# Banks of their own for the small products of a nested fast multiplication, with the products in another order

## The chip, the cores and the metric

The kernel runs on one core of a Trainium2 chip. The time is that of the device for one execution, in microseconds (us). The kernel before was run three times: 2297.75, 2298.81 and 2299.09 us, median 2298.81. The engines are TensorE (PE in the profile, its weight loads PEld), VectorE (DVE), ScalarE (ACT), GpSimd (POOL) and SyncE (SP), which here only issues transfers.

## The reference

An encoder of two layers takes one inference step for a prompt of 1024 rows and a sample of 32 rows, 1056 columns of 1024 features in the kernel. Layer one mixes with a matrix memory, layer two with windowed attention. Each is followed by a feed-forward block, which is where the change lies:

```
def swiglu(x, w_gu, w_down):
    g, u = jnp.split(x @ w_gu, 2, axis=-1)
    return (jax.nn.silu(g) * u) @ w_down

x = layer_norm(DEEPNORM_ALPHA * x + swiglu(x, w_gu[layer], w_down[layer]), ...)
```

The inner width is 2816. All is float32. The kernel splits every float32 number into a high part and a low part and makes three matmuls of each product (high by high, high by low, low by high).

## The kernel before

**The products.** The up projection has 22 units of 128 inner rows a layer (`FT`). Most are computed with a fast 2 x 2 block scheme: seven products in place of eight. Each product, called by the weight factor and the operand it multiplies, is 4 blocks deep, 2 column groups of 264 wide and 3 matmuls a block: 24 matmuls of 128 x 128 by 128 x 264. Its factors are a1, a2, b2, s2, s1, s3, s4. Four of them (a1, s2, s1, s4) add up in one PSUM tile, A, which ScalarE copies out between them (`gate0`, `up0`, `up1`, and last the silu); the others go to a tile B, which VectorE adds to `up0` or `up1`.

**The doubles.** Sixteen pairs of neighbouring units, 8 pairs a layer (`DOUBLES`, function `up_double`), go further: two units are rows 0 and 1, and the two a2 products are replaced by a second, nested scheme of seven small products of 6 matmuls each. They use four weights: g1 (a chain and a side product), g2 and g3 (a chain and a side product each) and g4 (a chain product). The chain products add up in one PSUM bank. A side product has the other bank. After each, VectorE adds the bank to a quarter of a gate (line 1582). Both banks are the halves of one tile, `inner`.

**Who orders what.** Each engine works through its own queue in the order in which the program is written. A planner, `Weights`, holds a list of jobs (`self.jobs`): one job makes one factor. VectorE forms the sum if there is one (lines 194 to 197 for g2; 212 for b2, 215 and 216 for s2, 218 for s1), ScalarE casts the high part (line 244), GpSimd subtracts for the low part (line 246). Five slots hold factors. When a product is done its slot is free, and jobs are made until four slots are taken (`done`), so jobs run about four ahead of the products. Raw weights (`wr`, line 172) are loaded on SP when the last job of a unit pair is made; the nested weights of the next double (`wn`, line 185) when the job g4 is made, since there is one buffer.

**The stage.** Results of finished unit pairs are prepared for the down projection by a generator, `stage`: it forms sums on VectorE, casts on ScalarE (line 1383), splits on GpSimd or VectorE (line 1384) and stores (line 1385, `hs_x` and `hs_t`). It is woven between the products by a clock of nominal times: each block of three matmuls ticks 0.339 us, and `yield` gives the time to the next step. `rest` and `finish_tile` do the same for the silu and the products that close a unit. The steps of the first stage sum are in lines 1395 and 1396, its cast follows after `yield 2.0`; a later step adds to a sum in line 1401.

**PSUM.** A and B are made by `bank`, which alternates two names a tag (`A0`, `A1`, `B0`, `B1`), two banks each, eight in all. In the doubles `B1` is `inner`.

Of the kernel before, what the change touches and what calls it, by code (L numbers as in the profile page):

```python
# [13 lines left out]
PSUM = bass.MemoryType.PSUM  # L14
DRAM = bass.MemoryType.DRAM

P = 128
# [112 lines left out]
class Weights:  # L130
# [7 lines left out]
    def __init__(self, nc, pool, units, pairs, doubles, on_vector):  # L138
        self.nc, self.pool, self.units, self.on_vector = nc, pool, units, on_vector
        self.nload = self.njob = 0  # L140
        self.raw, self.parts, self.home, self.live = {}, {}, {}, set()
        self.jobs, self.last = [], {}
        self.wait, self.ahead, self.pause = 0.0, False, FEED_W
        self.depth = RAW - 1
        self.doubles, self.inner, self.nest, self.nfetch = doubles, {}, None, 0
        self.spare, self.spared = None, set()
        u = 0
        while u < len(units):
            if u in doubles:
                v = u + 2  # L150
                self.jobs += [(u, f) for f in ("a1", "b2", "s2", "g1", "s1", "s3", "s4")]
                self.jobs += [(v, f) for f in ("a1", "b2")] + [(u, "g2"), (v, "s2"), (u, "g3")]
                self.jobs += [(v, f) for f in ("s1", "s3")] + [(u, "g4"), (v, "s4")]
                for i in range(4):
                    self.last[u + i] = len(self.jobs) - 1
                u += 4
            elif u in pairs:
                self.jobs += [(u, f) for f in self.FACTORS]
                self.last[u] = self.last[u + 1] = len(self.jobs) - 1
                u += 2  # L160
            else:
                self.jobs += [(u, 0), (u, 1)]
                self.last[u] = len(self.jobs) - 1
                u += 1
# [125 lines left out]
def kernel(ctx: ExitStack, tc: tile.TileContext, A, O):  # L290
# [1019 lines left out]
    def ffn(layer, li, tasks, lx, final):  # L1310
# [10 lines left out]
        AB = slice(0, 2)  # L1321
        px = ExitStack()

        turns = {"A": 0, "B": 0}

        def bank(tag, one=None):
            i = turns[tag] if one is None else one
            turns[tag] = 1 - i
            return new(px.pool[tag], f"{tag}{i}", [P, 2, 512])[:, :, :N4]

        X = seven(E)
        extras = ("t2", "t3", "t4")
# [39 lines left out]
        def stage(p):  # L1372

            (s11, s12), (s21, s22) = (kept.pop(2 * p + i) for i in range(2))
            s33, *pairs_ = places_
            m = s33 and buf(s33)
            pause = 5.2

            def put(o, s, eng, last=False):
                i = pairs_[turn[0]][0]  # L1380
                turn[0] ^= 1
                hi, lo = buf(i), buf(i + 1)
                nc.scalar.copy(hi.bitcast(F32R), buf(s))
                eng.tensor_sub(lo.bitcast(F32R), buf(s), hi)  # L1384
                nc.sync.dma_start(hs[o][:, p], buf2(i))
                if last:
                    release(s)

            if p in BLOCKS[TAIL]:
                for i, (o, s) in enumerate((("x11", s11), ("x12", s12), ("x21", s21), ("x22", s22))):  # L1390
                    put(o, s, (nc.gpsimd, nc.vector)[i % 2], True)
                    yield 4.0
                return

            nc.vector.tensor_sub(m, buf(s22), buf(s12))
            nc.vector.tensor_sub(buf(s12), buf(s12), buf(s11))
            yield 2.0
            put("t1", s12, nc.gpsimd, True)
            yield pause
            put("t3", s33, nc.vector)  # L1400
            nc.vector.tensor_add(m, m, buf(s11))
# [159 lines left out]

        def up_double(i):
            us = up[i], up[i + 1]
            inner = bank("B", 1)
            chain, side = inner[:, 0], inner[:, 1]
            gate0, up0, up1 = [None] * 2, [None] * 2, [None] * 2
            slot = [{}, {}]

# [32 lines left out]
            for row in range(2):  # L1601
                a = bank("A")
                mul(row, a, "a1", "x11")
                finish_tile()
                gate0[row] = take(row, "g0")
                nc.scalar.copy(gate0[row], a)
                if not row:
                    staging.append(wv.launch(stage(i // 2 - 1)))
                b = bank("B", 0)
                mul(row, b, "b2", "t4")  # L1610
                if row:
                    small(chain, "g2", 1, "t2", [(1, 0)], True, False)
                    small(side, "g2", 0, "t3", [(1, 1)])
                mul(row, a, "s2", "t2", again=True)
                up0[row] = take(row, "u0")
                nc.scalar.copy(up0[row], a)
                nc.vector.tensor_add(up0[row], up0[row], b)
                if row:
                    small(chain, "g3", 0, "t1", [(1, 1)], True, False)
                    small(side, "g3", 1, "t4", [(1, 0)], True)  # L1620
                else:
                    small(chain, "g1", 0, "x11", [(0, 0)], False, False)
                    small(side, "g1", 1, "x21", [(0, 0)])
                mul(row, a, "s1", "t1", again=True)
                up1[row] = take(row, "u1")
                nc.scalar.copy(up1[row], a)
                b = bank("B", 0)
                mul(row, b, "s3", "t3")
                nc.vector.tensor_add(up0[row], up0[row], b)
                nc.vector.tensor_add(up1[row], up1[row], b)  # L1630
                if row:
                    small(chain, "g4", 0, "x22", [(0, 1)], True)
                mul(row, a, "s4", "x22", again=True)
                nc.scalar.activation(take(row, "s1"), a, AF.Silu)
                tail.append(wv.launch(rest(row)))

# [74 lines left out]
        for i in range(FIRST, FT):  # L1711
            if i in DOUBLES:
                while nests:
                    wv.drain(nests.pop())
                up_double(i)
            elif i - 1 not in DOUBLES:
                if i == FIRST + 1:
                    open_nested()
                if i == DOUBLES.stop:
                    close_nested()  # L1720
# [529 lines left out]
```

## Time and profile before

| what | us |
|---|---|
| median of three runs | 2298.81 |
| profiled execution, its own time | 2297.69 |
| its span | 2295.9 |
| TensorE busy | 2188.7 |
| VectorE busy | 1534.3 |
| GpSimd busy | 1052.9 |
| ScalarE busy | 1020.0 |

A row of a timeline gives start, duration, engine, line, operation, out<-in and, in brackets, how long the engine had been idle and what ended that. A row of the waits gives who waited for whom, total us, times and the longest. A row of stretches gives the busy time of each engine between two moments, then the clock that TensorE was granted and the DMA's share and rate. Matmuls are pipelined: each shows about 0.28 us, but they start 0.12 us apart.

### The profile page before, as it was taken

Reading aid. Unit: us, or ns where it says so; the run is one execution under the profiler, and the core shown is the slowest. Engines: PE = TensorE matmul, PEld = TensorE weight load, DVE = VectorE, ACT = ScalarE, POOL = GpSimd, SP = SyncE. Lnnn points to the kernel's source line nnn. Section 1 sums busy time; section 2 is a strip of 40 time slices with the busy share of each in tenths; the row PEclk is TensorE's granted clock in tenths of the full one; section 3 lists DMA queues with packets and bytes.
Section 4 is the critical chain, followed back from the end, with each engine's and each line's share of the span. In section 5 each row is a group of like instructions: output and inputs, shape, how many; then the busy total and the mean of one; then the engine's idle time right before and its main releaser. Section 6 shows DMA issues by size and latency. Waiting matters only on the chain. (4 is left out here: it accounts for less than half of the span.)

```text
span 2295.9 us, 44506 instructions
## 1 busy us (share of the span) xinstructions
PE 2188.7 (95%) x16990; PEld 2150.8 (94%) x16990; DVE 1534.3 (67%) x3008; ACT 1020.0 (44%) x2299; POOL 1052.9 (46%) x1014
## 2 busy tenths in 40 slices
PE   9999999999898989999999999999889898999997
PEld 9999999999898989999998999899889898999997
DVE  4465677787576666566667778887766666556657
ACT  4443445464443434322246778665434343432224
POOL 2544200005665656454526777402565656554441
PEclk9999999999999999999999999999999999999999
DMA  4222214122434343697515434402443434399622
GB/s 164 76 59 68 59 31 142 28 83 98 155 134 159 129 144 146 231 336 244 179 66 170 118 90 114 156 27 93 141 153 130 144 136 158 113 347 302 209 83 76
DMA packets 181413, 315.15 MB, mean 137 GB/s; under 512 B 18832, under 2 KB 131528, under 8 KB 181200
## 3 DMA queue, kind: packets, MB, share of 16 engines
q1 hardware_dynamic: 176848, 307.98, 40.4%
q10 hardware_dynamic: 4352, 4.33, 0.6%
q8 instruction: 134, 2.20, 0.4%
q14 instruction: 79, 0.65, 0.1%
HBM read 214.51 MB, written 87.27 MB: 131 GB/s over the span
## 5 line engine op out<-in xcount | busy, mean ns | idle before, releaser
L246 POOL TENSOR_TENSOR wl_s<-wr,wh_s 128x512 fp32r<-128x512 f32 x224 | 317.6, 1433 | 282.8 <-ACT wh_s L244 219.9
L412 PE MATMUL d<-sx,wh 128*128 128x264 f32 (+2 forms) x1068 | 341.7, 320 | 2.5 <-ACT wh L244 2.4
L414 PE MATMUL d<-sx,wl 128*128 128x264 f32 (+2 forms) x1068 | 325.9, 305 | 2.3 <-POOL wl L246 2.3
L413 PE MATMUL d<-sx,wh 128*128 128x264 f32 (+2 forms) x1068 | 325.2, 304 | 0.4 <-DVE sx L443 0.4
L246 POOL TENSOR_TENSOR wl_a<-wr,wh_a 128x512 fp32r<-128x512 f32 x80 | 108.5, 1357 | 402.8 <-ACT wh_a L244 401.9
L244 ACT CAST wh_s<-wr 128x512 fp32r<-128x512 f32 x224 | 134.7, 618 | 317.3 <-DVE wr L216 257.9
L412 PE MATMUL A<-sx,wh_s 128*128 128x264 f32 x896 | 259.3, 289 | 2.7 <-ACT z L1467 2.7
L413 PE MATMUL A<-sx,wh_s 128*128 128x264 f32 x896 | 258.7, 289 | 0.0
L414 PE MATMUL A<-sx,wl_s 128*128 128x264 f32 x896 | 258.6, 289 | 0.0
L412 PEld LDWEIGHTS d<-sx,wh 128*128 128x128 f32 x1068 | 201.9, 189 | 6.0 <-ACT wh L244 3.2
L414 PEld LDWEIGHTS d<-sx,wl 128*128 128x128 f32 x1068 | 201.5, 189 | 3.7 <-POOL wl L246 3.4
L413 PEld LDWEIGHTS d<-sx,wh 128*128 128x128 f32 x1068 | 202.2, 189 | 1.6 <-DVE sx L443 0.7
L412 PE MATMUL d<-sx,ex 128*128 128x264 f32 x624 | 180.5, 289 | 0.1
L413 PE MATMUL d<-sx,ex 128*128 128x264 f32 x624 | 177.2, 284 | 0.0
L414 PE MATMUL d<-sx,ex 128*128 128x264 f32 x624 | 176.9, 284 | 0.0
L412 PEld LDWEIGHTS A<-sx,wh_s 128*128 128x128 f32 x896 | 173.1, 193 | 3.1 <-ACT z L1467 3.1
L414 PEld LDWEIGHTS A<-sx,wl_s 128*128 128x128 f32 x896 | 173.4, 194 | 0.0
L413 PEld LDWEIGHTS A<-sx,wh_s 128*128 128x128 f32 x896 | 173.2, 193 | 0.0
L246 POOL TENSOR_TENSOR wl<-wr,wh 128x512 fp32r<-128x512 f32 (+2 forms) x81 | 104.1, 1294 | 93.9 <-ACT wh L244 93.9
L1995 POOL TENSOR_SCALAR s<-s,st 128x256 f32<-128x256 f32 (+1 forms) x144 | 123.4, 870 | 43.8 <-DVE st L1993 31.1
L412 PE MATMUL A<-ex,wh_s 128*128 128x264 f32 x448 | 127.8, 285 | 2.0 <-ACT act L1457 2.0
L414 PE MATMUL A<-ex,wl_s 128*128 128x264 f32 x448 | 127.2, 284 | 0.5 <-POOL wl_s L246 0.5
(425 smaller groups left out, 7380.1 us busy)
## 6 DMA issues: line engine op xcount, KB each, us to landing
wr<-in_gu SPq DMA_DIRECT2D x92, 512.0 KB
hs_t<-act SPq DMA_DIRECT2D x64, 528.0 KB
hs_x<-act SPq DMA_DIRECT2D x56, 528.0 KB
sx<-hs_x SPq DMA_DIRECT2D x112, 264.0 KB
sx<-hs_t SPq DMA_DIRECT2D x64, 264.0 KB
ex<-hs_t SPq DMA_DIRECT2D x64, 264.0 KB
wr<-in_dn SPq DMA_DIRECT2D x32, 512.0 KB
hs_x<-z SPq DMA_DIRECT2D x16, 528.0 KB
```

Source lines behind the costliest of these rows:

```text
L244: self.nc.scalar.copy(hi, r)
L246: eng.tensor_sub(lo, r, hi.bitcast(F32))
L412: nc.tensor.matmul(out, ah, bh, start=start and k == 0, stop=False, **kw)
L413: nc.tensor.matmul(out, ah, bl, start=False, stop=False, **kw)
L414: nc.tensor.matmul(out, al, bh, start=False, stop=stop and k == last, **kw)
L1995: nc.gpsimd.tensor_scalar_mul(p[:R, h, lo:256], p[:R, h, lo:256], st[:R, 2, h : h + 1])
```

## The change

Four things are changed.

1. The two halves of `inner` become tiles of their own, `chain` and `side`. For that, the PSUM pools are closed and opened again at the first double and after the last, with one buffer of B in the doubles and two elsewhere (`side_banks`). `bank` takes a ring of buffers by one name instead of two names.
2. The order of the products in a double is other. Before, row 0: a1, b2, s2, g1 chain, g1 side, s1, s3, s4; row 1: a1, b2, g2 chain, g2 side, s2, g3 chain, g3 side, s1, s3, g4, s4. After, row 0: a1, g1 chain, g1 side, s2, b2, s1, s3, s4; row 1: a1, g2 chain, g2 side, s2, b2, s1, s3, g3 chain, g3 side, s4, g4. `finish_tile` comes after the copy `gate0`, not ahead of it.
3. The list of jobs follows that order, apart from b2, which stays ahead of s2, because the sum of s2 overwrites what b2 reads.
4. `yield 2.0` in the stage becomes `yield 3.6`.

```
-                self.jobs += [(u, f) for f in ("a1", "b2", "s2", "g1", "s1", "s3", "s4")]
-                self.jobs += [(v, f) for f in ("a1", "b2")] + [(u, "g2"), (v, "s2"), (u, "g3")]
-                self.jobs += [(v, f) for f in ("s1", "s3")] + [(u, "g4"), (v, "s4")]
+                self.jobs += [(u, f) for f in ("a1", "g1", "b2", "s2", "s1", "s3", "s4")]
+                self.jobs += [(v, "a1"), (u, "g2")] + [(v, f) for f in ("b2", "s2", "s1", "s3")]
+                self.jobs += [(u, "g3"), (v, "s4"), (u, "g4")]
...
-        turns = {"A": 0, "B": 0}
-
-        def bank(tag, one=None):
-            i = turns[tag] if one is None else one
-            turns[tag] = 1 - i
-            return new(px.pool[tag], f"{tag}{i}", [P, 2, 512])[:, :, :N4]
+        rings = {"A": 2, "B": 2}
+
+        def bank(tag):
+            return new(px.pool[tag], tag, [P, 2, 512], bufs=rings[tag])[:, :, :N4]
+
+        def side_banks(one):
+            px.close()
+            rings["B"] = 1 if one else 2
+            px.pool = {o: px.enter_context(pool("ps" + o, PSUM)) for o in "BA"}
...
-            yield 2.0
+            yield 3.6
             put("t1", s12, nc.gpsimd, True)
...
-            inner = bank("B", 1)
-            chain, side = inner[:, 0], inner[:, 1]
+            chain, side = (new(px.pool["B"], o, [P, 512])[:, :N4] for o in ("chain", "side"))
...
                 mul(row, a, "a1", "x11")
-                finish_tile()
                 gate0[row] = take(row, "g0")
                 nc.scalar.copy(gate0[row], a)
-                if not row:
-                    staging.append(wv.launch(stage(i // 2 - 1)))
-                b = bank("B", 0)
-                mul(row, b, "b2", "t4")
+                finish_tile()
                 if row:
                     small(chain, "g2", 1, "t2", [(1, 0)], True, False)
                     small(side, "g2", 0, "t3", [(1, 1)])
+                else:
+                    staging.append(wv.launch(stage(i // 2 - 1)))
+                    small(chain, "g1", 0, "x11", [(0, 0)], False, False)
+                    small(side, "g1", 1, "x21", [(0, 0)])
                 mul(row, a, "s2", "t2", again=True)
                 up0[row] = take(row, "u0")
                 nc.scalar.copy(up0[row], a)
+                b = bank("B")
+                mul(row, b, "b2", "t4")
                 nc.vector.tensor_add(up0[row], up0[row], b)
...
                 if row:
+                    small(chain, "g3", 0, "t1", [(1, 1)], True, False)
+                    small(side, "g3", 1, "t4", [(1, 0)], True)
+                mul(row, a, "s4", "x22", again=True)
+                if row:
                     small(chain, "g4", 0, "x22", [(0, 1)], True)
-                mul(row, a, "s4", "x22", again=True)
```

The order on the engines changes at three places, each shown in the third double of layer one. Names carry a running number; `[waits ...]` names the engines that an instruction waits for.

TensorE, at the step from the chain product of g1 to its side product, before:

```order
L413 MATMUL B_716_7971<-sx,wh_g_7966 128x264
L414 MATMUL B_716_7971<-sx,wl_g_7967 128x264
L412 MATMUL B_716_7971<-sx,wh_g_7966 128x264 [waits DVE_49]
L413 MATMUL B_716_7971<-sx,wh_g_7966 128x264
L414 MATMUL B_716_7971<-sx,wl_g_7967 128x264
```

and after:

```order
L413 MATMUL chain_7978<-sx,wh_g_7930 128x264
L414 MATMUL chain_7978<-sx,wl_g_7931 128x264
L412 MATMUL side_7979<-sx,wh_g_7930 128x264
L413 MATMUL side_7979<-sx,wh_g_7930 128x264
L414 MATMUL side_7979<-sx,wl_g_7931 128x264
```

The first matmul of the side product waits for VectorE before, and for nothing after.

ScalarE in row 0, from copy `up0` (line 1616, after the change 1618) past copy `up1` (1626, then 1624); `wh_a`, `wh_b` and `wh_s` are casts of the factors of row 1, `wh_g` that of g2. Before:

```order
L1616 COPY z_4632<-A_717_7972 128x528 [waits PE_49]
L244 CAST wh_a_8089<-wr_7857 128x512 [waits DMAHW0_49]
L1383 CAST act<-act 128x528 [waits DMAHW3_49]
L244 CAST wh_b_8123<-wr_7859 128x512 [waits DMAHW1_49,PE_49,Pool_49]
L1626 COPY z_4632<-A_717_7972 128x528 [waits PE_49]
L244 CAST wh_g_8157<-wn_7835 128x512 [waits DVE_49,Pool_49]
L1383 CAST act<-z_4632 128x528 [waits DMAHW4_49,Pool_49]
```

and after:

```order
L1618 COPY z_4632<-A_7980 128x528 [waits PE_49]
L244 CAST wh_a_8100<-wr_7846 128x512 [waits DMAHW6_49]
L1386 CAST act<-act 128x528 [waits DMAHW3_49]
L244 CAST wh_g_8137<-wn_7879 128x512 [waits DVE_49,PE_49]
L1624 COPY z_4632<-A_7980 128x528 [waits PE_49]
L244 CAST wh_b_8168<-wr_7848 128x512 [waits DMAHW7_49,Pool_49]
L1386 CAST act<-z_4632 128x528 [waits DMAHW4_49,Pool_49]
```

The cast of g2, which waits for VectorE, stood behind copy `up1` and stands ahead of it; the cast of b2 went the other way.

SP near the end of a double, from one store of the stage to the next, before:

```order
L1385 DMA hs_x_79<-act 128x1056 [waits DMAHW5_49,Pool_49]
L185 DMA wn_7835<-in_gu 128x512 [waits DMAHW6_49,Pool_49]
L185 DMA wn_7835<-in_gu 128x512 [waits DMAHW7_49]
L172 DMA wr_7857<-in_gu 128x1024 [waits DMAHW0_49,DVE_49]
L172 DMA wr_7859<-in_gu 128x1024 [waits DMAHW1_49,Pool_49]
```

and after:

```order
L1388 DMA hs_x_79<-act 128x1056 [waits DMAHW5_49,Pool_49]
L172 DMA wr_7846<-in_gu 128x1024 [waits DMAHW6_49]
L172 DMA wr_7848<-in_gu 128x1024 [waits DMAHW7_49,Pool_49]
L185 DMA wn_7879<-in_gu 128x512 [waits DMAHW0_49,Pool_49]
L185 DMA wn_7879<-in_gu 128x512 [waits DMAHW1_49]
```

The nested weights of the next double were issued ahead of two raw loads, and are issued behind them.

More of the change, by code (lines that the diff above doesn't have):

```diff
@@ L1616, in up_double @@
                 nc.scalar.copy(up0[row], a)
+                b = bank("B")
+                mul(row, b, "b2", "t4")
                 nc.vector.tensor_add(up0[row], up0[row], b)
[L1618 to L1623, printed above, removed]
                 mul(row, a, "s1", "t1", again=True)
@@ L1626, in up_double @@
                 nc.scalar.copy(up1[row], a)
-                b = bank("B", 0)
+                b = bank("B")
                 mul(row, b, "s3", "t3")
@@ L1714, in ffn @@
                     wv.drain(nests.pop())
+                if i == DOUBLES.start:
+                    finish_tile()
+                    side_banks(True)
                 up_double(i)
@@ L1719, in ffn @@
                 if i == DOUBLES.stop:
+                    finish_tile()
+                    side_banks(False)
                     close_nested()
```

## The prediction

> **What bounds the kernel now.** I read the page's head first, then the waits of TensorE, then stretches of the paired feed-forward units, and last single rows of four queues.
>
> ```profile
> span 2295.9 us, 44506 instructions
> PE 2188.7 (95%) x16990; PEld 2150.8 (94%) x16990; DVE 1534.3 (67%) x3008; ACT 1020.0 (44%) x2299; POOL 1052.9 (46%) x1014
> ```
>
> TensorE is busy 95% of the span and every other engine at most 67%. The instruction count of TensorE does not change, so time can only come from its idle 107 us and from its clock. Who makes it wait (total us, times, longest):
>
> ```profile
> PE B L412 <- DVE z L1582: 45.8, 34, 4.4
> PE B L412 <- DVE act L1582: 22.0, 14, 2.3
> PE A L412 <- ACT z L1467: 2.7, 2, 1.3
> ```
>
> Two rows hold 67.8 us in 48 waits; the next one is 2.7 us. All 48 wait for line 1582, the VectorE add that reads a small product out of tile B. There are 16 doubles (8 a layer), so three waits each: the three places where a side product follows a chain product directly. Next, two stretches of one double each, then the whole paired stretch of either layer (length, then busy us by engine, granted clock, DMA):
>
> ```profile
> core 0: us, PE busy (x) PEld busy (x) DVE busy (x) ACT busy (x) POOL busy (x), PEclk, DMA share, GB/s
> 603.56:648.92 45.36, 40.88 (x331) 40.23 (x330) 30.27 (x37) 18.12 (x34) 28.09 (x20) 1.00 0.39 141
> 574.14:920.00 345.86, 312.53 (x2477) 307.64 (x2476) 218.99 (x269) 137.69 (x250) 210.97 (x153) 0.98 0.40 144
> 1644.00:1990.00 346.00, 313.60 (x2495) 308.49 (x2493) 223.31 (x272) 138.31 (x252) 211.58 (x153) 0.99 0.41 145
> ```
>
> A double takes 45.4 us. VectorE is busy 30.3 of them and GpSimd 28.1, so if TensorE needed only 40 us they would still be at 76% and 70%: no engine becomes the bound by its sum; only the order in the queues can. Now TensorE's own rows: one wait, a product of 24 matmuls without one, and the first wait of the layer with what follows.
>
> ```profile
> 669.68 0.28 PE L414 MATMUL B<-sx,wl_g 128*128 128x264 f32 x1
> 672.28 0.39 PE L412 MATMUL B<-sx,wh_g 128*128 128x264 f32 x1 [2.32 <-DVE act L1582]
> 672.50 0.28 PE L413 MATMUL B<-sx,wh_g 128*128 128x264 f32 x1
> ...
> 627.73 0.28 PE L412 MATMUL A<-sx,wh_s 128*128 128x264 f32 x1
> 630.65 0.28 PE L412 MATMUL B<-ex,wh_s 128*128 128x264 f32 x1
> ...
> 579.38 0.59 PE L412 MATMUL B<-sx,wh_g 128*128 128x264 f32 x1 [4.36 <-DVE z L1582]
> 585.46 0.29 PE L412 MATMUL A<-sx,wh_s 128*128 128x264 f32 x1
> ```
>
> A product of 24 takes 630.65 - 627.73 = 2.92 us, 0.122 us a matmul; a small one of 6 takes 0.73. A double has 12 x 24 + 7 x 6 = 330 matmuls, 40.2 us without waits. From 669.68 to 672.28 are 2.60 us instead of 0.12, and the next step is 0.22 instead of 0.12: a wait shown as 2.32 costs 2.58, so 0.26 more than it shows. After the 4.36 us wait the 28 matmuls up to 585.46 take 6.08 us instead of 3.4: half speed, 2.7 us lost.
>
> **Part 1, the small products get banks of their own.** A side product then no longer waits for the add of the chain product before it (the order of TensorE in the part on the change shows the wait gone). Removed: 67.8 + 48 x 0.26 = 80.3 us. With the waits the slow clock goes: (1 - 0.98) x 345.86 + (1 - 0.99) x 346 = 6.9 + 3.5 = 10.4 us by the two stretches. Together 90.7 us, 4%: the most that can be had here. [...]
>
> The cover that goes: the wait also held TensorE back until VectorE and ScalarE had caught up. What is late next is asked at each place where TensorE reads something within few products.
>
> **Part 2, the order of products, and what ScalarE's queue makes of it.** TensorE now does a1, small ones, s2, b2, s1, s3, s4. Tile A is added to again by s2, s1 and s4, each only after ScalarE has copied it out. The s4 product follows s1 by one product (2.92 us). In the order of ScalarE the cast of g2 now stands before that copy (up1), and the cast waits for four VectorE subtractions (L194 to L197), which stand behind two staging steps. VectorE and ScalarE today:
>
> ```profile
> 622.86 0.71 DVE L1396 TENSOR_TENSOR act<-act,z 128x528 f32<-128x528 f32 x1
> 625.80 0.70 DVE L1617 TENSOR_TENSOR z<-z,B 128x528 f32<-128x528 f32 x1 [2.23 <-ACT z L1616]
> 626.42 0.42 DVE L1582 TENSOR_TENSOR z<-z,B 128x264 f32<-128x264 f32 x1
> 628.28 1.64 DVE L1384 TENSOR_TENSOR act<-act 128x528 fp32r<-128x528 f32 x1
> 629.95 1.67 DVE L1401 TENSOR_TENSOR act<-act,z 128x528 f32<-128x528 f32 x1
> 632.15 0.41 DVE L194 TENSOR_TENSOR wn<-wn 128x256 f32<-128x256 f32 x1
> 633.51 0.43 DVE L197 TENSOR_TENSOR wn<-wn 128x256 f32<-128x256 f32 x1
> ...
> 606.04 0.70 DVE L1384 TENSOR_TENSOR act<-act 128x528 fp32r<-128x528 f32 x1
> ```
>
> ```profile
> 623.60 0.63 ACT L1383 CAST act<-act 128x528 fp32r<-128x528 f32 x1 [4.87 <-DVE act L1396]
> 624.14 1.13 ACT L244 CAST wh_s<-wr 128x512 fp32r<-128x512 f32 x2
> 625.18 0.59 ACT L1616 COPY z<-A 128x528 f32<-128x528 f32 x1
> 630.85 0.60 ACT L1626 COPY z<-A 128x528 f32<-128x528 f32 x1 [2.37 <-PE A L414]
> 633.57 0.62 ACT L244 CAST wh_g<-wn 128x512 fp32r<-128x512 f32 x1 [2.12 <-DVE wn L196]
> ```
>
> Today the copy runs at 630.85, 0.2 us after its product, and the cast comes 2.7 us later and holds nobody. After the change, counted from the end of b2: the add starts at 0.2 and takes 0.62 to the next start; the staging split 1.67, the staging add 1.67, the four subtractions 633.94 - 632.15 = 1.79: 5.95. Cast and copy, about 0.6 each, end at 7.15. TensorE wants s4 after s1 and s3, at 5.84. So it waits 1.3 us. If the split takes 0.70 as at 606.04, it waits 0.35; if a semaphore's step is lost here and there, 1.6. I take 1.3, since 1.64 is what the split took at this place. It applies to 14 doubles (the last of a layer stages without these steps): 14 x 1.3 = 18 us, between 5 and 22. [...]
>
> The wait of g2's cast for a chain product costs nothing: between two uses of the chain bank lies at least one product of 2.92 us, and the add takes 0.42. Copy gate0 before s2 has 1.46 us of small products as cover and takes 0.2 + 0.6; its ScalarE queue is free by then. finish_tile behind that copy moves no ScalarE work that TensorE awaits. On VectorE the two adds of g1 now stand ahead of the up0 add and wait for their products; both products end before b2, for which the up0 add waits anyway.
>
> **Part 3, the later casts of the first staged sums.** Today L1383 waits 4.87 us for the sum of L1396 and copy up0 (625.18) stands behind it; that is why the first wait of a double is 2.3 us where the mean is 67.8 / 48 = 1.4. With 3.6 for 2.0 the cast still stands ahead of the copy, but s2 ends later: count from the end of the double's last s4. A cast and the silu end at 1.4; VectorE then has a product of 1.63, two of 1.79 and three sums of 0.7, so the staged sum is ready near 8.5; its cast, another cast and the copy, 0.6 each, end near 10.4. s1 wants the copy at 0.73 + 2.92 + 1.46 + 2.92 + 2.92 = 10.95. Nothing, with 0.5 us to spare.
>
> ```profile
> 616.54 1.63 DVE L1590 TENSOR_TENSOR act<-act,z 128x528 f32<-128x528 f32 x1 [1.97 <-ACT act L1634]
> 618.10 1.79 DVE L1597 TENSOR_TENSOR z<-z 128x528 f32<-128x528 f32 x1
> ```
>
> **Part 4, the inner weights are fetched last and used first.** On SP, the two loads of wn now stand behind two of wr. Today:
>
> ```profile
> 691.75 0.32 SPq L1385 DMA_DIRECT2D hs_x<-act  x1
> 692.45 0.93 SPq L185 DMA_DIRECT2D wn<-in_gu  x2
> 693.47 3.01 SPq L172 DMA_DIRECT2D wr<-in_gu  x2
> ...
> 691.70:701.20 9.50, 8.46 (x69) 8.25 (x69) 4.01 (x6) 3.39 (x6) 4.23 (x5) 1.00 0.81 279
> ```
>
> ```profile
> 690.40 1.32 POOL L1384 TENSOR_TENSOR act<-act 128x528 fp32r<-128x528 f32 x1
> 691.68 0.73 POOL L246 TENSOR_TENSOR wl_g<-wn,wh_g 128x256 fp32r<-128x256 f32 x1
> ```
>
> Count from the start of row 1. Copy up0 ends at 8.1, the x21 cast at 8.7, GpSimd's split at 10.0 (1.32): hs_x is issued, wr behind it, and wn when GpSimd has done s4 (1.3) and g4 (0.73), at 12.1. The 2.1 MB ahead and with it move at 279 GB/s: 7.5 us, wn is there at 17.8. Then ScalarE casts g1 and, behind it, b2; GpSimd splits both; VectorE's sum for s2 and its cast follow, at 22.4; the silu of row 1's s4 stands behind that cast and ends about 1 us later than in part 3. This pushes the chain of part 3 past its 0.5 us to spare and the gate0 copy of the next double past its cover: about 0.8 us a double, 14 times: 11 us. It is 0 if the data come 1 us sooner, 35 if they come 2 us later (2.5 each).
>
> **Part 5, the ends of the paired stretch.** The first g1 cast of a layer now stands ahead of copy up1 of the unit before, and waits for the first wn:
>
> ```profile
> 562.47 0.28 PE L412 MATMUL A<-sx,wh_s 128*128 128x264 f32 x1
> ...
> 561.63 0.80 SPq L185 DMA_DIRECT2D wn<-in_gu  x2
> 560.05 0.59 ACT L1474 COPY act<-A 128x528 f32<-128x528 f32 x1
> ```
>
> 0.5 MB at 279 GB/s is 1.9 us: landed near 563.5, cast and copy to 564.7, and s4 wants it where it starts today, at 562.5. 2 us, between 0 and 4, twice: 4 us. The stage before the first double still has casts that wait for their stores ahead of copy up0: of the 4.36 us I leave 2 a layer, 4 us. Closing and opening the PSUM pools adds no wait on the first a1; I cost it at nothing, since the tiles under it were read a product earlier. New waits may cost some clock: 2 us.
>
> **Sum.** -90.7 + 18 + 11 + 4 + 4 + 2 = -52, against the profiled execution's 2297.7 (span 2295.9): 2246. The median of the runs is 1.1 above that: 2247.
>
> **The rivals.** (a) Nothing takes the place of the waits: splits run at 0.70, wn comes in time. Then 2298.8 - 90.7 + about 5 = 2213. For it: every engine has a fifth of its time free. Against: the 1.64 at this very place. (b) wn comes 2 to 3 us later: 28 to 42 us less gain, 2275 to 2289. For it: its load is now the last of four in one queue, and ScalarE stands behind it. (c) Slower: the same place, but each us that wn comes later than 17.8 costs 14 us; from 52 / 14 = 3.7 us on, at 21.5, the gain is gone, and at 22 the time is 2306. It needs the 2.1 MB to take 11.2 us instead of 7.5, 188 GB/s, or the issue to come that much later; against it stands the measured 279. (d) The split of the tiles does nothing, because the adds are awaited anyway: within 0.2% (4.6 us, about what a measurement here can tell from no change). Against it: the side products carry no wait in the order.
>
> **How the numbers follow.** Forecast 0.60 (2225 to 2272 by the ends of parts 2 to 5), (a) 0.13, (b) 0.14, (c) 0.09, (d) 0.04. Faster 0.87, same 0.04, slower 0.09. The range runs from (a)'s 2213 to into (b), 2284: it leaves out (c), (d) and the far ends of (b) and the forecast.
>
> **What the changed profile would show.** Part 1: no TensorE wait on line 1584 worth naming, doubles of 41.5 to 42.5 us, clock 1.00. Part 2: waits of A on ScalarE's copy at line 1624, about 14 of 1.3 us. Part 4: ScalarE's g casts waiting for the wn load. Wrong it is if tile A waits for other copies by several us a double, or if small products wait for g weights.

## The result, and the profile after

The changed kernel takes 2264.18 us (median of four runs, 2261.38 to 2265.36), the kernel before 2298.51 us beside it (2297.75 to 2299.09). The ratio is 0.9849, 95% interval 0.9832 to 0.9866: 1.5% faster, 34 us. The forecast was 2247, its range 2213 to 2284. The profiled execution of the changed kernel has a span of 2261.8 us, 34.1 less than before. Its page begins:

```profile
span 2261.8 us, 44523 instructions
PE 2185.3 (97%) x16990; PEld 2147.7 (95%) x16990; DVE 1567.8 (69%) x3008; ACT 1015.0 (45%) x2299; POOL 1077.7 (48%) x1014
```

TensorE's idle time fell from 2295.9 - 2188.7 = 107.2 us to 2261.8 - 2185.3 = 76.5 us, by 30.7. Its busy time fell by only 3.4. The waits of TensorE in the changed kernel (total us, times, longest) for ScalarE's copies out of tile A:

```profile
PE A L412 <- ACT z L1607: 14.7, 10, 3.0
PE A L412 <- ACT act L1607: 7.9, 6, 1.5
PE A L412 <- ACT z L1624: 5.4, 10, 2.0
PE A L412 <- ACT z L1470: 4.5, 2, 2.3
PE A L412 <- ACT act L1477: 4.1, 2, 3.1
PE A L412 <- ACT z L1618: 3.0, 10, 0.3
PE A L412 <- ACT act L1624: 1.1, 4, 0.3
PE A L412 <- ACT act L1618: 0.9, 3, 0.3
```

The 48 waits for the VectorE add (line 1582 before, 1584 now) are gone to the last one. In their place stand waits for ScalarE's copies out of tile A: `gate0` (L1607, 16 times, 22.6 us: one in each double), `up1` (L1624, 14 times, 6.5), `up0` (L1618, 13 times, 3.9), and at the entry of each layer's paired stretch the copies of the plain unit ahead of it (L1470, L1477). Two steady doubles, from one s2 of row 0 to the next:

```profile
620.84:663.88 43.04, 40.94 (x331) 40.31 (x331) 31.13 (x37) 17.83 (x34) 29.60 (x21) 1.00 0.42 150
663.88:706.54 42.66, 40.80 (x331) 40.18 (x331) 32.09 (x37) 17.82 (x34) 30.12 (x21) 1.00 0.42 152
```

A double takes 42.7 to 43.0 us at full clock; it took 45.4. The forecast named 41.5 to 42.5. What happens inside one of them, by single rows of SyncE, ScalarE, VectorE, GpSimd and TensorE:

```profile
647.19 1.79 SPq L172 DMA_DIRECT2D wr<-in_gu  x2
649.24 0.82 SPq L185 DMA_DIRECT2D wn<-in_gu  x2
654.99 0.62 ACT L244 CAST wh_g<-wn 128x512 fp32r<-128x512 f32 x1 [3.33 <-DMA wn<-in_gu]
657.36 1.29 POOL L246 TENSOR_TENSOR wl_b<-wr,wh_b 128x512 fp32r<-128x512 f32 x1
658.68 0.69 DVE L216 TENSOR_TENSOR wr<-wr,wr 128x512 f32<-128x512 f32 x1 [2.42 <-POOL wl_b L246]
659.46 0.62 ACT L244 CAST wh_s<-wr 128x512 fp32r<-128x512 f32 x1 [3.33 <-DVE wr L216]
661.41 1.78 POOL L1387 TENSOR_TENSOR act<-act 128x528 fp32r<-128x528 f32 x1
663.22 0.60 ACT L1607 COPY act<-A 128x528 f32<-128x528 f32 x1 [0.53 <-POOL act L1387]
663.88 0.39 PE L412 MATMUL A<-ex,wh_s 128*128 128x264 f32 x1 [1.49 <-ACT act L1607]
...
689.90 0.41 ACT L244 CAST wh_g<-wn 128x256 fp32r<-128x256 f32 x1 [1.07 <-PE B L413]
697.07 0.62 ACT L244 CAST wh_g<-wn 128x512 fp32r<-128x512 f32 x1 [2.49 <-DMA wn<-in_gu]
705.88 0.60 ACT L1607 COPY z<-A 128x528 f32<-128x528 f32 x1 [0.53 <-POOL act L1387]
```

Read downward to the matmul, each row waits for one above it or stands behind it in a queue. The nested weights `wn` are issued behind two loads of `wr`. The cast of g1 waits 3.33 us for them and holds ScalarE. GpSimd splits g1 and then b2. The sum of s2 (L216) overwrites what the split of b2 reads, so it waits for that. The cast of s2 waits for the sum. The last staging split (L1387) follows in GpSimd's queue, behind the split of s2. The copy `gate0` waits for that split, because it is written into the staging slot that the split has just read. Only then may s2 add to tile A. Then the loop closes: the products run on, the cast of g4 waits for a slot that a B product of row 1 frees (689.90), and with it the next nested weights are fetched. From one copy `gate0` to the next it is 26.7 us (663.22 to 689.90) + 7.2 (to 697.07) + 8.8 (to 705.88) = 42.7: the length of a double.

The entry of layer two shows the same on a larger scale, where the first nested weights of a layer are awaited:

```profile
1618.16 0.62 ACT L244 CAST wh_g<-wn 128x512 fp32r<-128x512 f32 x1 [3.62 <-DMA wn<-in_gu]
1619.34 0.39 PE L412 MATMUL A<-sx,wh_s 128*128 128x264 f32 x1 [0.96 <-ACT act L1477]
1621.44 1.79 DVE L1411 TENSOR_TENSOR z<-z,act 128x528 f32<-128x528 f32 x1 [5.50 <-POOL act L1387]
1627.17 0.62 ACT L244 CAST wh_s<-wr 128x512 fp32r<-128x512 f32 x1 [6.83 <-DVE wr L216]
1629.88 0.39 PE L412 MATMUL A<-ex,wh_s 128*128 128x264 f32 x1 [2.98 <-ACT z L1607]
```

The cast waits 3.62 us. That holds the copy behind it (0.96 us of TensorE), and it holds GpSimd too, whose next staging split VectorE awaits for 5.50 us; VectorE then gives s2's sum late, ScalarE stands 6.83 us for it, and the first copy `gate0` is 2.98 us late.

### The profile page after: what moved, and what is told of

Read it like the earlier page. It is cut to its first block, busy times and chain, and to the rows that moved or that the text cites. A ratio compares the mean times of both kernels' runs of the same rounds, so it can differ in the third digit from the quotient of the medians.

```text
span 2261.8 us, 44523 instructions
## 1 busy us (share of the span) xinstructions
PE 2185.3 (97%) x16990; PEld 2147.7 (95%) x16990; DVE 1567.8 (69%) x3008; ACT 1015.0 (45%) x2299; POOL 1077.7 (48%) x1014
## 4 chain that ended last, share of the span: by engine, by line
PE 63%; DVE 15%; ACT 7%; issue 6%; DMA 5%; POOL 4%; SPq 0%; POOLq 0%; ACTq 0%; DVEq 0%
PE d L412 9%; PE d L414 9%; PE d L413 9%; PE A L412 6%; PE A L414 6%; PE A L413 6%; PE B L412 4%; PE B L413 4%; PE B L414 4%; DMA wn<-in_gu 2%; DVE z L1599 1%; PE T L2021 1%; POOL wl_b L246 1%; DVE wr L218 1%; ACT act L515 1%
## 5 line engine op out<-in xcount | busy, mean ns | idle before, releaser
L246 POOL TENSOR_TENSOR wl_s<-wr,wh_s 128x512 fp32r<-128x512 f32 x224 | 329.1, 1488 | 203.6 <-ACT wh_s L244 152.2
L412 PEld LDWEIGHTS A<-sx,wh_s 128*128 128x128 f32 x896 | 169.9, 190 | 26.0 <-ACT z L1624 7.5
L413 PEld LDWEIGHTS A<-sx,wh_s 128*128 128x128 f32 x896 | 170.0, 190 | 0.0
L246 POOL TENSOR_TENSOR wl_g<-wn,wh_g 128x512 fp32r<-128x512 f32 x64 | 92.9, 1452 | 80.4 <-ACT wh_g L244 78.9
```

Of the source, the lines that this page charges most:

```text
L246: eng.tensor_sub(lo, r, hi.bitcast(F32))
L412: nc.tensor.matmul(out, ah, bh, start=start and k == 0, stop=False, **kw)
L413: nc.tensor.matmul(out, ah, bl, start=False, stop=False, **kw)
```

## The experiments

Theory 1, from that reading: the late nested weights set the pace, through what is queued behind the cast of g1. Theory 2: in the new order the copies lack cover, whenever the weights come. A third question is how much of 34 us comes from the banks and how much from the order, which here means points 2 to 4 of the change together: products, jobs and the longer pause.

**The banks alone.** The kernel before, its order, its jobs and its pause, with the new `bank`, `side_banks`, and

```
-            inner = bank("B", 1)
-            chain, side = inner[:, 0], inner[:, 1]
+            chain, side = (new(px.pool["B"], o, [P, 512])[:, :N4] for o in ("chain", "side"))
```

> The kernel before with part 1 alone: chain and side banks of their own, B one tile deep, the products, the jobs and the staging pause as before. The step of the prediction (banks take 80 us of waits and 10 us of clock away, the new order gives some 40 of them back): the old order keeps copies gate0 and up0 with a whole outer product of cover, so no new wait of tile A worth 0.5 us a double appears and the time is 2208 to 2225 us. Rival, the order is needed to collect the gain: in the old order the casts of the first staged sums and the g casts now make the copies late, waits of A of 2 us a double appear in place of the side waits, and the time is 2255 us or more.

Measured: 2223.29 us, ratio 0.9673 (0.9659 to 0.9686). The banks alone gain 74 us, more than twice the whole change. Its page head, its first two waits, and one double:

```profile
span 2218.8 us, 44524 instructions
PE 2168.1 (98%) x16990; PEld 2137.9 (96%) x16990; DVE 1554.8 (70%) x3008; ACT 1015.6 (46%) x2299; POOL 1080.4 (49%) x1014
```

```profile
PE A L412 <- ACT z L1618: 6.0, 10, 1.0
PE A L412 <- ACT act L1618: 4.5, 4, 1.9
```

```profile
659.22:700.09 40.87, 40.36 (x330) 40.15 (x331) 30.87 (x37) 17.88 (x34) 29.79 (x21) 1.00 0.46 158
```

TensorE's idle time is 50.7 us, 56.5 less than before, and its busy time 20.6 less. By an estimate from the rows and the clocks, some 9 us of that are the 34 waits fewer, each with 0.27 us beyond what it shows, and 11 the granted clock, 0.997 over this span for 0.992 before. A double takes 40.9 us against a floor of 40.2. One wait is left in the doubles, 14 times, 10.5 us: the copy `up0` of row 0. The time is inside the expected range, at its upper end; that no new wait of 0.5 us a double would appear did not hold, since this one is 0.75 us a double on average (1.9 and 1.6 in the first of a layer, near 0.5 in most others).

**The order alone.** The changed kernel with the two banks as halves of one tile again:

```
-            chain, side = (new(px.pool["B"], o, [P, 512])[:, :N4] for o in ("chain", "side"))
+            inner = new(px.pool["B"], "inner", [P, 2, 512])[:, :, :N4]
+            chain, side = inner[:, 0], inner[:, 1]
```

> The changed kernel with chain and side again as the halves of one tile; order, jobs and the later cast as changed. If the banks carry the gain, 48 waits for the VectorE adds of the small products (line 1584) are back with about 68 us shown, and the new waits on ScalarE's copies shrink, since TensorE comes later to them: 2290 to 2335 us, no faster than the kernel before. If the order carries a part of its own, the time stays below 2285 us.

Measured: 2407.72 us, ratio 1.048 (1.0465 to 1.0494), far beyond both expectations. The first two waits:

```profile
PE inner L412 <- DVE z L1585: 92.4, 34, 8.7
PE inner L412 <- DVE act L1585: 49.2, 14, 6.8
```

The 48 waits are back, and twice as long as before (141.6 us for 67.8). With 2298, 2223, 2408 and 2264 us the four corners are known: the new order costs 110 us without the banks and 41 with them, and the banks gain 74 us in the old order and 144 in the new. So the order carries no gain of its own. The new order puts the small product g1 where VectorE is still busy with the unit before: in one double the add of g1's chain product (685.28) stands behind the products of line 1593 and 1600, the sum of s1 and two staging sums, 7.75 us together, and TensorE waits 6.52 us for it. That is why the split of the tiles matters more in this order.

**The nested weights sooner.**

```
-                self.jobs += [(u, "g3"), (v, "s4"), (u, "g4")]
+                self.jobs += [(u, "g3"), (u, "g4"), (v, "s4")]
```

> The changed kernel with job g4 ahead of the last s4 in the list, so that SyncE issues the two loads of the nested weights ahead of the two loads of the next raw weights. Theory 1 (the nested weights come late, the cast of g1 holds ScalarE, and with it b2, the sum of s2, its cast, the x22 split and so the copy gate0): the cast of g1 waits under 1 us for the load instead of 3.3, s2 no longer waits for copy gate0 (1.0 to 1.5 us shown, 1.6 real, 12 to 13 times) and 15 to 22 us go: 2242 to 2250 us. Theory 2 (the copy gate0 has too little cover in this order, whenever the weights come): the cast waits less, the wait of s2 stays above 1 us, and the time is within 5 us of the changed kernel's 2264.

Measured: 2246.31 us, ratio 0.9775 (0.9762 to 0.9788), 18 us below the changed kernel. In the same place as above, a cast of g1:

```profile
650.10 0.62 ACT L244 CAST wh_g<-wn 128x512 fp32r<-128x512 f32 x1 [1.19 <-PE B L413]
```

It no longer waits for the load but 1.2 us for a product that frees its slot, and the waits for `gate0` fall from 22.6 us to 8.4: 3.0 in the first double of either layer, and 0.15 to 0.19 in each of the other 14. That is theory 1's time, and its wait is nearly gone.

**The nested weights later.** Each load issued twice:

```
-        for i in range(2):
+        for i in (0, 1, 0, 1):
```

> The changed kernel with each nested weight loaded twice over in a row, so that it is there later by the time of 0.5 MB, 1.9 us at the 279 GB/s that was measured, or by more, as the second pair waits for the first. Theory 1 (the nested weights set the pace, and each us costs a us a double): the cast of g1 waits 2 us or more longer, and with 12 steady doubles and two entries 1.9 x 14 = 27 us or more are lost: 2285 to 2320 us. Theory 2 (the late weights are no cause, the copies lack cover): within 6 us of 2264.

Measured: 2298.09 us, ratio 1.0004 (0.9995 to 1.0013): the whole gain of the change is lost. One turn of the loop on ScalarE (copy `gate0`, cast of g4, cast of g1; the copy `gate0` that ends it starts at 711.44):

```profile
667.09 0.60 ACT L1607 COPY act<-A 128x528 f32<-128x528 f32 x1 [0.51 <-POOL act L1387]
693.77 0.41 ACT L244 CAST wh_g<-wn 128x256 fp32r<-128x256 f32 x1 [1.07 <-PE B L413]
703.63 0.62 ACT L244 CAST wh_g<-wn 128x512 fp32r<-128x512 f32 x1 [5.17 <-DMA wn<-in_gu]
711.44 0.60 ACT L1607 COPY z<-A 128x528 f32<-128x528 f32 x1 [0.52 <-POOL act L1387]
```

26.7 + 9.9 + 7.8 = 44.4 us. Beside the changed kernel's 26.7 + 7.2 + 8.8 = 42.7 the first piece is the same to 0.01 us; the piece with the load grew by 2.7, of which the piece behind it took back 1.0. Beyond that 1.0 us the loop has no slack. Theory 2 (no more than 6 us) falls.

**The same load, with less queued behind it.** One swap, so that the cast of g1 no longer stands ahead of b2 and s2:

```
-                self.jobs += [(u, f) for f in ("a1", "g1", "b2", "s2", "s1", "s3", "s4")]
+                self.jobs += [(u, f) for f in ("a1", "b2", "g1", "s2", "s1", "s3", "s4")]
```

> The changed kernel with one swap in the list of jobs: b2 of row 0 ahead of g1. The nested weights are loaded as late as in the changed kernel, but the cast of g1 no longer stands ahead of b2, the sums and the cast of s2 on ScalarE, nor their splits on GpSimd. Theory 1 (the late load hurts only through what stands behind the cast of g1): the waits for gate0 go (17 us with what they do not show), and at the entry of each layer the waits for the copy up1 (3.1 and 1.0 us) and for the first copy gate0 (1.5 and 3.0 us) shrink to under 1: 2228 to 2240 us. Rival (the load itself is too late for g1's product): small products now wait for the weights of g1, and the time is 2255 us or more.

Measured: 2239.15 us, ratio 0.9746 (0.9732 to 0.9759), 25 us below the changed kernel. The load is issued as late as in the changed kernel, yet:

```profile
PE A L412 <- ACT z L1624: 6.3, 10, 2.0
PE A L412 <- ACT z L1618: 2.8, 10, 0.3
PE A L412 <- ACT z L1607: 1.8, 3, 1.4
```

The waits for `gate0` are down to 2.2 us (these 1.8, and 0.4 for copies into the other staging tile), those for L1477 are gone, and a double takes 41.5 us. So the late load harms through ScalarE's and GpSimd's queues, not through g1's own product.

**The entries alone.** The same swap for the first double of each layer only.

```
-                self.jobs += [(u, f) for f in ("a1", "g1", "b2", "s2", "s1", "s3", "s4")]
+                first = not self.doubles.index(u) % len(DOUBLES)
+                self.jobs += [(u, f) for f in ("a1", *(("b2", "g1") if first else ("g1", "b2")), "s2", "s1", "s3", "s4")]
```

> The changed kernel with b2 ahead of g1 in the list of jobs for the first double of either layer only; the other 14 doubles keep the changed order. It prices the entries, to which the prediction gave 4 us for the late first load: by that about 2260 us. By the traces some 15 us are lost there (waits of 3.1 and 1.0 us for copy up1 of line 1477, of 1.5 and 3.0 for the first copy gate0, and matmuls at a lower clock behind them): 2248 to 2254 us. The steady doubles keep their wait for gate0.

Measured: 2256.39 us, ratio 0.9818 (0.9805 to 0.9832). The entries cost 8 us, between the forecast's 4 and the 10 to 16 expected from the trace; the other 17 of the swap's 25 us belong to the steady doubles.

**Two waits that were taken away for nothing.** First the staging slot that `gate0` waits for:

```
-            i = free.pop(0)
+            i = free.pop(1 if other and len(free) > 1 else 0)
...
-                s = slot[row][name] = alloc()
+                s = slot[row][name] = alloc(name == "g0" and not row)
```

> The changed kernel with one choice changed: the copy gate0 of row 0 takes the second free slot of the staging buffer instead of the first, which is the one that the last split of the staging (x22, GpSimd, line 1387) has just read. Theory 1 says that this split is late as everything behind the nested weights is; without the tie the copy comes 0.5 us sooner, and 0.5 x 13 = 7 us go: about 2257 us, a wait of about 0.7 us at s2 staying. Theory 3 (the tie to that slot is the whole of the new wait): the wait of s2 goes, and the time is about 2245 us.

Measured: 2262.05 us, ratio 0.9844 (0.983 to 0.9857), no different from the changed kernel; neither theory's number. Then the cast of g2 put behind the copy `up1`:

```
-                self.jobs += [(v, "a1"), (u, "g2")] + [(v, f) for f in ("b2", "s2", "s1", "s3")]
+                self.jobs += [(v, "a1"), (v, "b2"), (u, "g2")] + [(v, f) for f in ("s2", "s1", "s3")]
```

> The changed kernel with one swap in the list of jobs: b2 of row 1 ahead of g2, so that the cast of g2 goes to ScalarE behind copy up1 of row 0 and no longer ahead of it. The prediction priced what this cast does to s4 at 18 us (1.3 a double), so 2246 us. The trace of the changed kernel shows 0.3 us of wait for line 1624 in a steady double, 0.58 by its step, and 2.0 and 1.0 in the first doubles: by that 8 us, so 2256 us. If the wait of s2 grows instead, nothing: 2264 us.

Measured: 2262.45 us, ratio 0.9844 (0.9831 to 0.9858), the same. In the second of them the waits for L1624 did go, and the others are:

```profile
PE A L412 <- ACT z L1607: 18.5, 11, 3.0
PE A L412 <- ACT act L1607: 9.1, 6, 1.7
```

27.6 us for `gate0` instead of 22.6: what TensorE no longer waited for `up1` it waited there. In the first, the waits moved from L1607 (14.4 left) to L1618 (12.0). Both are what a loop that sets the pace looks like: TensorE reaches the next step of the loop sooner, and the step comes when it comes.

**All three swaps of the list.** b2 ahead of g1, b2 ahead of g2, g4 ahead of the last s4.

> The changed kernel with three swaps in the list of jobs: b2 ahead of g1 in row 0, b2 ahead of g2 in row 1, g4 ahead of the last s4. If what the new order of products costs is all in ScalarE's and SyncE's queues, the waits for gate0, for up1 at line 1624 (0.6 us a double with what is not shown) and at the entries go together, and the time comes to that of the banks alone, 2218 to 2230 us. If the new order of the products itself lacks cover, whatever the jobs do, waits of 1 us a double stay and the time is 2235 us or more.

Measured: 2232.87 us, ratio 0.9717 (0.9704 to 0.9731), between the two expectations. With the loop broken the swap of g2 and g4 does count: 6 us less than the swap of b2 alone. What is left of the doubles' waits:

```profile
PE A L412 <- ACT z L1607: 5.7, 4, 1.7
PE A L412 <- ACT z L1618: 2.8, 10, 0.3
PE A L412 <- ACT act L1618: 1.1, 4, 0.3
```

A double takes 41.3 us, 0.45 more than with the banks alone. The four waits of L1607 stand in the first double of each layer, one a row; the 14 for `up0` (0.3 shown) are in every staged one, for in the new order the copy `up0` still stands behind a staging cast. So of the 41 us that the order cost, the three swaps give back 31. Of the 10 that stay, the waits for `up0` are 7.8 with their steps; that much of theory 2 holds.

**The later cast.** In the changed kernel back to 2.0:

```
-            yield 3.6
+            yield 2.0
```

> The changed kernel with the first pause of the stage back at 2.0. By the prediction the later cast does nothing, 2264 us. By the trace it moves the casts of the stage in the plain units too, where the wait for copy up0 of line 1470 grew from 1.3 to 2.3 us in either layer: undone, 2 to 7 us less, about 2260 us. If the later cast is needed in the doubles (copy up0 of row 0 behind a cast that waits), waits of 0.5 to 1 us for line 1618 appear and the time is 2268 to 2278 us.

Measured: 2266.35 us, ratio 0.986 (0.9847 to 0.9874): no difference that can be told. The wait of line 1470 went from 2.3 to 1.3 us a layer, and a wait of 2.2 us for L1618 came in the first double of layer one; those for copies of the plain unit ahead grew as well (L1477 from 4.1 to 6.1 us in all, and 2.0 new for L1460). In the banks-only kernel, a pause long enough to put the cast behind the copy (the last of the staged casts left where it was):

```
-            pause = 5.2
+            pause = 4.4
...
-            yield 2.0
+            yield 6.2
```

> The banks alone (old order) with the first staged cast put behind the copy up0 of row 0: the first pause of the stage 6.2 for 2.0 and the others 4.4 for 5.2, so that the stage ends where it did. In the banks-only run the one wait that is left in the doubles is for the copy up0, 14 times, 10.5 us shown and about 15 real. If it is the cast that waits for the staged sum ahead of that copy, the wait goes and the time is 2205 to 2214 us. If something else makes the copy late, it stays at 2219 to 2226 us.

Measured: 2218.44 us, ratio 0.9655 (0.9641 to 0.9668). A hundred us of doubles, and the largest wait for a copy that is left:

```profile
600.00:700.00 100.00, 99.96 (x818) 99.38 (x817) 75.00 (x91) 44.66 (x83) 71.47 (x49) 1.00 0.48 163
```

```profile
PE A L412 <- ACT z L1470: 6.1, 2, 3.1
```

The waits for `up0` are gone from the steady doubles, where TensorE is idle for 0.04 us in 100. The time lies between the two expectations. Against the banks alone TensorE's idle time fell by 7.9 us, to 42.8, but its busy time rose by 5.9, and the granted clock went from 0.997 to 0.995. Some of the gain was lost in the plain units ahead of the doubles, where the longer pause put a cast ahead of the copy of line 1470: 3.4 us more wait, and in layer one a stretch of 3.5 us at half speed behind it. What else made TensorE busier was not followed up. Last, the longer pause for the stages in the doubles alone (`yield 6.2 if p else 2.0`, `pause = 4.4 if p else 5.2`):

> As the banks with the later cast, but the later pauses only for the stages that are launched in the doubles; the stage launched in the plain units ahead of them keeps 2.0 and 5.2. With the later pauses everywhere the doubles ran without a wait, but copy up0 of the plain unit ahead of the doubles (line 1470) came 3.1 us late in either layer, against 1.3 with the old pauses. If that is the pauses' doing in that unit, two waits shrink by 1.8 us and the slow matmuls behind them go: 2208 to 2214 us. If it comes from elsewhere, 2216 to 2220 us.

Measured: 2217.83 us, ratio 0.9653 (0.964 to 0.9666). The wait of line 1470 is back at 1.3 us, as expected, and the time is no lower: TensorE's busy time fell by 3.8 us, but its idle time rose by 2.3, part of it in waits of the first doubles for `chain` and B (0.5 us each) and for line 1460 (1.0 a layer). This is the fastest version, 46 us below the changed kernel and no different from the one with the longer pause everywhere.

## Why the prediction came out as it did

The direction and the cause of the gain were right, and the two copies at which most time was lost were named. The loss was larger than forecast, and most of it lay at the other of the two: `gate0`, not `up1`. That the sum still came within 17 us is in part luck, since part 2 was 12 us too dear and made up for some of the 28 that the other terms left out. Shown waits count with 0.28 us more each (TensorE's rows around the new waits of the steady doubles show 0.26 to 0.28), and by the rows of the changed kernel:

| term | predicted us | measured us |
|---|---|---|
| Part 1: 48 waits gone | -80.3 | -80.3, none left |
| clock (10.4 won, 2 lost) | -8.4 | about -3.4 (busy time 2188.7 to 2185.3) |
| Part 2: s4 waits for `up1`; stage ahead of the first doubles (part 5) | +18 + 4 | +10.4 (6.5 shown, 14 times) |
| Part 3: `up0` behind the staged cast | 0 | +7.5 (3.9 shown, 13 times) |
| Part 4: late nested weights, `gate0` of the other 14 doubles | +11 | +22.1 (18.2 shown) |
| Part 5: entries | +4 | +8.9 |
| sum | -52 | -34.8 (spans: -34.1) |

**Part 1** was right to the wait: line 1584 holds nobody. As a change by itself it gave 74 us of its 90.7; 10.5 shown, 14.4 with their steps, went to the copy `up0`, which is late next in the old order, and with the staged cast out of its way the gain was 79 to 80. The clock came back with the banks alone (granted 0.997 over the whole span against 0.992), not with the whole change (0.994). The 10.4 us were right: the kernel before has six stretches at half speed among the paired units, some 100 matmuls that start 0.22 us apart and not 0.12, and the double shown of the banks alone ran at a granted clock of 1.00. The changed kernel has three, 45 matmuls, each of them behind a wait of 2.3 to 3.1 us at an entry. So new waits there cost 4.5 us of clock, where 2 were forecast.

**Part 2** named the right wait (s4, line 1624, 14 times) at 1.3 us; the steady ones measure 0.3 shown, 0.57 by the step. Two things shorten it: the staging split behind `up0` took 1.05 us there and not 1.64, and TensorE was itself 0.6 us late, from its wait for `up0`. The same part said that copy `gate0` has 1.46 us of cover and that "its ScalarE queue is free by then". That sentence is the step that failed: the queue was not free. It was held by the cast of s2 (3.33 us for its sum), with five more instructions behind it (659.99 to 662.70). The copy also waited for GpSimd's last staging split, whose slot it reuses, a tie that the prediction did not have; but taking only the tie away, in the run with the other slot, gained nothing.

**Part 4** had the mechanism, and the size wrong: its 0.8 us a double for `gate0` is the term that was too small. The weights were there 18.4 us into row 1 of the double shown, against 17.8 worked out, and the cast of s2 ended at 23.4, against 22.4. Measured are 22.1 us in 14 doubles, 1.6 each, inside the 0 to 35 that were given as its bounds. What was missing lies between that cast and the copy: the five instructions on ScalarE, and on GpSimd the split of s2 (1.30 us) and the staging split (1.78). The swap of b2 measures this term without adding up waits: 17 us in the steady doubles, of the 22.1.

**Part 3** said that the later cast does nothing, with 0.5 us to spare. Undone, it changes nothing; but the spare was not there, and 13 doubles wait 0.3 us for that copy. One of the "three sums of 0.7" is line 218, ahead of the staged sum in VectorE's queue. It took that time at this place before, and takes 1.1 us more after (the first row is of the kernel before):

```profile
621.53 0.68 DVE L218 TENSOR_TENSOR wr<-wr,wr 128x512 f32<-128x512 f32 x1
```

```profile
665.39 1.77 DVE L218 TENSOR_TENSOR wr<-wr,wr 128x512 f32<-128x512 f32 x1
```

The silu ahead of that chain also came late, behind the cast of s2. But the waits for `up0` are not the late weights' doing alone: they stay where those for `gate0` are nearly gone, 12 times with the weights sooner and 14 times with the swap of b2, 0.3 us each. The later cast also moved a cast in the plain unit, for 1 us of line 1470 a layer, which was not foreseen.

**Part 5** took 2 us a layer for the first cast of g1 waiting ahead of copy `up1`; the runs give 4 (8.9 us by the rows: 4.7 for line 1477, 5.0 for the first copies `gate0`, 1.8 more for line 1470, 2.6 less for line 1457 of before). It counted ScalarE's queue only. GpSimd and VectorE stood as well, up to the first copy `gate0`.

The range that the forecast gave itself from the ends of parts 2 to 5, 2225 to 2272, is not their sum, which is 2219 to 2279; 2264 lies in both.

Of the rivals, (a), nothing in place of the waits, is nearly what the banks alone do (2213 against 2218 with the cast moved); it needed the old order. (b) had the right place, with a load later than it was. Rival (c) took 14 us for each us that the weights come later, and said that 3.7 us would use up the gain. The load issued twice bears that out in kind: with the piece of the loop that holds the load 2.7 us longer, the time is that of the kernel before. (d) is excluded by the banks alone.

## What to carry to other kernels

When a wait is removed, ask of each thing that the next step reads whose queue it is in, and follow that queue through every engine: a cast that waits for a load (here 3.33 us) holds not only its own engine but the splits and sums behind it, and these free the buffers that the next copy needs. Where the trace shows a loop (a buffer's release, a load, a cast, a copy, and the products that lead to the release), only what shortens the loop counts; two waits of TensorE taken away elsewhere gave nothing (2262 us each, for 2264) until the loop was broken by one swap in a list. And measure the parts of a change one by one: here one of them held all of the gain, and the others took back more than half of it.

## What the runs showed of the hardware

The clock did not fall by the length of a wait alone. In the changed kernel one place of either layer has nearly the same wait, and behind it:

```profile
556.68 0.39 PE L412 MATMUL A<-sx,wh_s 128*128 128x264 f32 x1 [2.25 <-ACT z L1470]
1610.78 0.59 PE L412 MATMUL A<-sx,wh_s 128*128 128x264 f32 x1 [2.28 <-ACT z L1470]
```

```profile
1610.78:1613.80 3.02, 3.02 (x13) 3.02 (x14) 2.32 (x3) 0.94 (x2) 1.48 (x1) 0.50 0.80 246
556.68:559.70 3.02, 3.02 (x25) 3.02 (x26) 2.32 (x3) 0.93 (x2) 1.49 (x1) 1.00 0.82 255
```

In layer two 13 matmuls in 3 us at a granted clock of 0.50, in layer one 25 at 1.00. With the entries swapped, a wait of 1.97 us was followed by half speed from 585.07 to 588.49, at a granted clock of 0.51 in the first 3 us:

```profile
585.07 0.54 PE L413 MATMUL A<-sx,wh_s 128*128 128x264 f32 x1 [1.97 <-ACT z L1625]
...
588.49 0.32 PE L413 MATMUL A<-sx,wh_s 128*128 128x264 f32 x1
```

That half speed lasted 3.42 us. In the kernel before, five of the six stretches lasted 3.30 to 3.47 us; the one behind the 4.36 us wait was longer (28 matmuls in 6.08 us). Of that kernel's twelve waits of 2.28 to 2.33 us in the paired units, four have half speed 0.8 to 1.5 us behind them, and eight have none. With the banks and the longer pause everywhere, 3.06 us was followed by half speed in layer one (558.27 to 561.74), and 3.07 us at the same place of layer two was not: the granted clock was 1.00 in the 3 us behind it. What decides, these runs don't settle.

The other surprise is that the same instructions took longer after the change. VectorE's 3008 instructions took 1534.3 us before and 1567.8 after, GpSimd's 1014 took 1052.9 and 1077.7. Line 218 shows it most plainly. Its 56 sums took 1123 ns on average before and 1419 after, and around the paired units each single one takes either 0.68 or near 1.8 us. It isn't that TensorE waited less: with the banks alone it waits less still (50.7 us idle for 76.5), and the mean is 1143 ns. What differs around the paired units is the neighbour. Of the single rows of line 218 there in the changed kernel, the 31 that lie mostly beside a GpSimd instruction take 1.78 us on average and the 7 others 0.68. Before, 16 lie beside one, at 1.71 (one of them at 0.68), and 19 do not, at 0.68. A neighbour does not always go with 1.8 us: in the plain units behind, 16 rows of either kernel lie mostly beside a GpSimd instruction and take 0.69 to 1.21 us. This is a reading of rows; no run moved one split by itself to test it. It does advise care with a duration taken from a trace of before: line 218 changed by 1.1 us at one place without any change to the instruction.
